# Strassen's scheme for the gate and up projections of two SwiGLU stages

## The chip, the cores and the metric

The kernel runs on one core of a Trainium2 chip. The metric is the device time of one execution in microseconds (us), the median of several runs; smaller is better. A core has a matrix engine (TensorE, PE in the rows; PEld is its loading of weights), VectorE (DVE), ScalarE (ACT), GpSimd (POOL) and SyncE (SP, which here issues most transfers). Each engine works through its own list of instructions in order, and a semaphore holds an instruction until what it reads is there and what it overwrites has been read. Matmuls write PSUM, which has 8 banks of 128x512 fp32; everything else lies in SBUF.

## The reference, cut to what matters

```python
def _swiglu_ffn(x, g_norm, w_gate_up, w_down):
    h = _rms_norm(x, g_norm)
    gate, up = jnp.split(h @ w_gate_up, 2, axis=-1)
    return (jax.nn.silu(gate) * up) @ w_down
...
    for layer in range(DEPTH):
        if layer < N_A:
            x = x + _gmlp_mixer(...)
        else:
            x = x + _chunked_relbias_attention(...)
        x = x + _swiglu_ffn(x, ffn_norm[layer], ffn_w_gate_up[layer], ffn_w_down[layer])
    return _rms_norm(x, final_norm)
```

There are two layers, 1024 tokens, a model width of 1024 and a hidden width of 2816; all is fp32. Layer 0 has the gMLP mixer ahead of its SwiGLU, layer 1 has chunked attention ahead of its SwiGLU.

## The kernel before

The residual stream `x` lies transposed in SBUF: eight tiles `x[d]`, each 128 features by 1024 tokens. A product in fp32 is made of three fp32r matmuls: each operand is split into a rounded part (`hi`, a copy by ScalarE) and the rest (`lo`, a subtraction by VectorE), and `hi*hi`, `hi*lo` and `lo*hi` are summed in PSUM (`split`, line 116; `mm_cols`, line 194; `mm_rows`, line 209).

A SwiGLU stage (`ffn`, line 463) works by blocks `f` of 128 hidden features, 22 of them. For each it multiplies the eight `h` tiles (scaled `x`, split once at the stage's start by `norm_input`, line 185) by a 128x1024 block of gate weights (`wg`) and one of up weights (`wup`). One block is 8 tiles of K x 2 halves of the tokens x 3 matmuls of 128x512, which is 48 for gate and 48 for up. `post` then multiplies both by the broadcast reciprocal norm `rbc` (lines 507 and 510), applies SiLU and the product (lines 514 and 515), and splits the result `y`. After every second `f` the down projection of an earlier pair of blocks runs: 16 units of 6 matmuls, each of which VectorE adds to `x` (line 219). The last pair in layer 0 runs in `rows_late` (line 443; its matmuls are line 455), and the last four blocks in layer 1 run with the final norm.

Weights come through `prep_w` (line 93): a transfer of 512 KB on SP's queue into one of two `wraw` buffers, a split into one of four `whi`/`wlo` pairs, and then `take_w` hands them out in the order of a list. The squares for the norm (`square_add`, line 137) are made by ScalarE and summed by GpSimd (line 149). The norm's own statistics use small fp32 matmuls (lines 169 and 181). The instructions of each engine are ordered by the framework's scheduler and not by the order of the code, so what stands where is shown below from the built programs.

## Time and profile before

| what | value |
|---|---|
| median of 3 runs | 2639.02 us (2638.77 to 2643.23) |
| the profiled execution's own time | 2636.19 us |
| its span in the profile | 2634.4 us |
| TensorE busy | 2578.9 us, 98% of the span |
| VectorE, ScalarE, GpSimd busy | 1456.9, 774.9 and 212.9 us |
| mean granted TensorE clock | 0.994 of full speed |
| moved by transfers | 161.35 MB, 61 GB/s on average |

The span runs from the first to the last instruction of the profile; the execution's own time lies 1.8 us above it, and the median of the runs another 2.8 us above that. The matrix engine's busy time counts overlapping matmuls once, so it says that the engine always has one in flight, not how many finish in a microsecond; for that one counts starts.

### The profile page before, as it was taken

To read this page: it belongs to the slowest core of one execution; us is meant where nothing else is said; L and a number is where in the kernel's file an instruction comes from. 1 tells how busy PE (TensorE), PEld (TensorE's weight loads), DVE (VectorE), ACT (ScalarE), POOL (GpSimd) and SP (SyncE) were. 2 spreads that over 40 slices of the span, in tenths; PEclk is the share of its full clock that TensorE was granted. 3 is DMA by queue.
4 is the path that set the end of the run, shared out by engine and by line. 5 is a ranking of instruction groups with operands and counts; after the bars stand their busy time and mean duration, and the time that the engine had idled before them with its cause. 6 is when DMAs were issued, how large, how long until landed. Compare 5 with 4: busy or idle time off the path is not lost.

```text
span 2634.4 us, 30026 instructions
## 1 busy us (share of the span) xinstructions
PE 2578.9 (98%) x12150; PEld 2138.2 (81%) x12150; DVE 1456.9 (55%) x2388; ACT 774.9 (29%) x1275; POOL 212.9 (8%) x155
## 2 busy tenths in 40 slices
PE   8999999999999999999999999989999999999998
PEld 6888888878888888888777888868888888888887
DVE  6237676774444444444657777788744444444435
ACT  5223322332111111111345555554421111111113
POOL 3001211130000000000410100030200000000001
PEclk9999999999999999999999999999999999999999
DMA  5232222211111111111112222222211111111111
GB/s 192 80 120 68 77 65 68 68 41 41 48 49 48 48 49 48 48 49 49 58 53 67 59 64 59 79 73 70 72 40 49 48 48 48 49 48 48 49 48 64
DMA packets 70538, 161.35 MB, mean 61 GB/s; under 512 B 6016, under 2 KB 34688, under 8 KB 70400
## 3 DMA queue, kind: packets, MB, share of 16 engines
q1 hardware_dynamic: 68096, 155.24, 18.6%
q10 hardware_dynamic: 2304, 4.20, 0.5%
q8 instruction: 95, 1.56, 0.3%
q14 instruction: 43, 0.35, 0.0%
HBM read 134.25 MB, written 16.78 MB: 57 GB/s over the span
## 4 chain that ended last, share of the span: by engine, by line
PE 90%; DVE 5%; ACT 2%; issue 1%; DMA 1%; POOL 1%; DVEq 0%; SPq 0%; ACTq 0%; POOLq 0%
PE ps L204 43%; PE ps L218 22%; PE pj L204 7%; PE pj L218 3%; PE ps L334 2%; PE ps L332 2%; PE ps L333 2%; PE po L756 2%; PE pt L729 2%; PE s L706 1%; PE ps L455 1%; PE s L709 1%; DVE p L713 1%; DVE p L721 1%; DVE kd L675 1%
## 5 line engine op out<-in xcount | busy, mean ns | idle before, releaser
L204 PE MATMUL ps<-hhi,whi 128*128 128x512 f32 x1664 | 655.4, 394 | 0.0
L204 PE MATMUL ps<-hlo,whi 128*128 128x512 f32 x1664 | 648.8, 390 | 2.8 <-DVE hlo L134 2.8
L204 PE MATMUL ps<-hhi,wlo 128*128 128x512 f32 x1664 | 648.2, 390 | 0.0
L117 ACT CAST whi<-wraw 128x1024 fp32r<-128x1024 f32 (+1 forms) x213 | 219.7, 1045 | 1218.2 <-PE ps L204 558.3
L204 PEld LDWEIGHTS ps<-hhi,wlo 128*128 128x128 f32 x1664 | 312.4, 188 | 66.1 <-issue 0.5
L204 PEld LDWEIGHTS ps<-hlo,whi 128*128 128x128 f32 x1664 | 312.9, 188 | 65.4 <-DVE hlo L134 4.1
L204 PEld LDWEIGHTS ps<-hhi,whi 128*128 128x128 f32 x1664 | 312.4, 188 | 61.0 <-issue 0.5
L118 DVE TENSOR_TENSOR wlo<-wraw,whi 128x1024 fp32r<-128x1024 f32 (+1 forms) x213 | 262.9, 1245 | 59.5 <-ACT whi L117 59.4
L510 DVE TENSOR_TENSOR ub<-ps,rbc 128x512 f32<-128x512 f32 x88 | 60.3, 691 | 339.3 <-PE ps L204 339.3
L219 DVE TENSOR_TENSOR x<-x,ps 128x512 f32<-128x512 f32 x272 | 182.5, 684 | 116.2 <-PE ps L218 116.1
L218 PE MATMUL ps<-yhi,whi 128*128 128x512 f32 x544 | 212.6, 391 | 0.0
L218 PE MATMUL ps<-yhi,wlo 128*128 128x512 f32 x544 | 211.7, 389 | 0.0
L218 PE MATMUL ps<-ylo,whi 128*128 128x512 f32 x544 | 211.7, 389 | 0.0
L507 DVE TENSOR_TENSOR ga<-ps,rbc 128x512 f32<-128x512 f32 x88 | 60.3, 691 | 255.4 <-PE ps L204 255.4
L204 PE MATMUL pj<-hhi,whi 128*128 128x512 f32 x368 | 152.9, 415 | 2.0 <-DVE x L458 2.0
L204 PE MATMUL pj<-hlo,whi 128*128 128x512 f32 x368 | 148.2, 403 | 0.7 <-DVE hlo L118 0.7
L204 PE MATMUL pj<-hhi,wlo 128*128 128x512 f32 x368 | 147.8, 402 | 0.0
L219 DVE TENSOR_TENSOR xb<-xb,ps 128x512 f32<-128x512 f32 (+1 forms) x160 | 103.6, 658 | 71.4 <-PE ps L218 71.0
L105 POOL TENSOR_TENSOR wraw<-wraw,gv 128x1024 f32<-128x1024 f32 x24 | 46.4, 1934 | 1014.2 <-DMA wraw<-wv_att 724.5
L218 PEld LDWEIGHTS ps<-yhi,wlo 128*128 128x128 f32 x544 | 102.1, 188 | 21.3
L218 PEld LDWEIGHTS ps<-ylo,whi 128*128 128x128 f32 x544 | 102.2, 188 | 20.7
L218 PEld LDWEIGHTS ps<-yhi,whi 128*128 128x128 f32 x544 | 102.1, 188 | 20.7
(408 smaller groups left out, 4024.0 us busy)
## 6 DMA issues: line engine op xcount, KB each, us to landing
wraw<-wg SPq DMA_DIRECT2D x44, 512.0 KB, 3.3
wraw<-wup SPq DMA_DIRECT2D x44, 512.0 KB, 3.3
wraw<-wd SPq DMA_DIRECT2D x44, 512.0 KB, 3.4
vd<-vt SPq DMA_DIRECT2D x32, 256.0 KB, 2.5
wraw<-wu SPq DMA_DIRECT2D x16, 512.0 KB, 3.5
wraw<-wout SPq DMA_DIRECT2D x16, 512.0 KB, 3.3
vr<-vd SPq DMA_DIRECT2D x32, 256.0 KB, 3.1
wraw<-wv SPq DMA_DIRECT2D x15, 512.0 KB, 3.4
```

What stands on the lines that cost most here:

```text
L117: self.nc.scalar.copy(hi, src)
L118: self.nc.vector.tensor_tensor(lo, src, hi.bitcast(F32), ALU.subtract)
L204: nc.tensor.matmul(ps[s], wt[:, c], ht[:, t], start=(kt == 0 and i == 0), stop=(kt == KT - 1 and i == 2),)
L218: nc.tensor.matmul(o, wt[:, c], yt[:, t], start=(j == 0 and i == 0), stop=(j == last and i == 2))
L219: nc.vector.tensor_tensor(x[d][:, t], x[d][:, t], o, ALU.add)
L332: nc.tensor.matmul(ps[tt], hhi[:, t], whi[:, c], start=(kt == 0), stop=False)
L333: nc.tensor.matmul(ps[tt], hhi[:, t], wlo[:, c], start=False, stop=False)
L334: nc.tensor.matmul(ps[tt], hlo[:, t], whi[:, c], start=False, stop=(kt == KT - 1))
L507: nc.vector.tensor_tensor(t, g[s], rbc[:, c], ALU.mult)
L510: nc.vector.tensor_tensor(b, u[s], rbc[:, c], ALU.mult)
L729: nc.tensor.transpose(tp[:, i * P:(i + 1) * P], pt[:, i * P:(i + 1) * P], self.ident)
L756: nc.tensor.matmul(o, vt[:, kb, j, :], r, start=(i == 0), stop=(i == len(jobs) - 1))
```

## The change

Gate and up of one block `f` are taken as one product of a 2x2 block matrix of weights with a 2x2 block matrix of activations. The rows of the weight matrix are gate (A11, A12) and up (A21, A22), its columns the even and the odd K tiles; the activations are split into even and odd K tiles (rows) and the two halves of the tokens (columns: B11, B12, B21, B22). Winograd's form of Strassen's scheme then makes the four results from seven products in place of eight, with S1 to S4 (sums of weight blocks), T1 to T4 (sums of activation blocks), and sums of the products. The host stores the weights with even K tiles first (`cols2`).

For each `f`, GpSimd makes S1 and S2 (tile `s12`) and S3 and S4 (`s34`) in four operations of 128x512; three and a half tiles of 128x1024 are split in place of two. The seven products have 12 matmuls each, in three PSUM banks; where the scheme sums two products they accumulate in one bank, and ScalarE and VectorE read the bank between them. VectorE makes the remaining sums in four tiles `ac`, `bu`, `gg`, `yy`. The result `y` goes to memory (`yd`).

At the start of a stage `x` goes to memory (`xd`), and `b_tiles` makes seven split tiles of each pair of `x` tiles. The first block (`f` = 0) runs as these tiles come, with seven banks. After the last `f`, `y` and `x` come back from memory and the whole down projection runs as a second pass, with the same matmuls as before. The three matmuls of a product read their operands in the same way as `mm_cols`.

```diff
+    def scratch(self, name, dtype=F32):
+        return self.hx.tile([P, S], dtype, name=name, tag="scr", bufs=3)
...
+    def quad_split(self, q, key, src):
+        w = src.shape[1]
+        hi = self.wp.tile([P, 1024], F32R, name="whi", bufs=self.NW)
+        lo = self.wp.tile([P, 1024], F32R, name="wlo", bufs=self.NW)
+        self.split(hi[:, 0:w], lo[:, 0:w], src)
+        for i, k in enumerate(key):
+            q[k] = (hi[:, i * 512:(i + 1) * 512], lo[:, i * 512:(i + 1) * 512])
...
+    def quad_s12(self, q):
+        nc = self.nc
+        g, u = q["raw"]
+        s12 = self.scratch("s12")
+        nc.gpsimd.tensor_tensor(s12[:, HALF[0]], u[:, HALF[0]], u[:, HALF[1]], ALU.add)
+        nc.gpsimd.tensor_tensor(s12[:, HALF[1]], s12[:, HALF[0]], g[:, HALF[0]], ALU.subtract)
+        q["s12"] = s12
+        self.quad_split(q, ("S1", "S2"), s12)
+    def quad_a(self, q):
+        self.quad_split(q, ("A11", "A12"), q["raw"][0])
+    def quad_s34(self, q, s34=None, split=True):
+        nc = self.nc
+        g, u = q["raw"]
+        s34 = s34 or self.scratch("s34")
+        nc.gpsimd.tensor_tensor(s34[:, HALF[0]], g[:, HALF[0]], u[:, HALF[0]], ALU.subtract)
+        nc.gpsimd.tensor_tensor(s34[:, HALF[1]], g[:, HALF[1]], q["s12"][:, HALF[1]], ALU.subtract)
+        q["s34"] = s34
+        if split:
+            self.quad_split(q, ("S3", "S4"), s34)
+    def quad_a22(self, q):
+        self.quad_split(q, ("A22",), q["raw"][1][:, HALF[1]])
...
+    def b_tiles(self, B, i, xe, xo, ge, go):
+        nc = self.nc
+        t1, t2 = HALF
+        e = self.scratch(f"e{i}")
+        t = self.scratch(f"t{i}")
+        names = {k: self.slot(j, f"b{k}_{i}") for k, j in (
+            ("eh", i), ("el", 4 + i), ("oh", 8 + i), ("ol", 12 + i), ("th", 16 + i), ("tl", 20 + i), ("t4", 24 + i))}
+        eh, el, oh, ol, th, tl, t4 = (names[k] for k in ("eh", "el", "oh", "ol", "th", "tl", "t4"))
+        stt = nc.vector.scalar_tensor_tensor
+        nc.scalar.activation(e, xe, AF.Copy, scale=ge)
+        nc.vector.tensor_tensor(t[:, t1], e[:, t2], e[:, t1], ALU.subtract)
+        stt(t[:, t2], xo[:, t2], go, t[:, t1], ALU.mult, ALU.subtract)
+        stt(e[:, t2], xo[:, t2], go, e[:, t2], ALU.mult, ALU.subtract)
+        self.split(eh, el, e)
+        self.split(th, tl, t)
+        nc.scalar.activation(oh, xo, AF.Copy, scale=go)
+        stt(ol, xo, go, oh.bitcast(F32), ALU.mult, ALU.subtract)
+        stt(e[:, t1], xo[:, t1], go, t[:, t2], ALU.mult, ALU.subtract)
+        self.split(t4[:, t1], t4[:, t2], e[:, t1])
+        for k, (h, l, c) in {"B11": (eh, el, t1), "T3": (eh, el, t2), "B21": (oh, ol, t1), "B22": (oh, ol, t2),
+                             "T1": (th, tl, t1), "T2": (th, tl, t2)}.items():
+            B[k, i] = (h[:, c], l[:, c])
...
+    def product(self, ps, A, B, pairs, start, stop, goes_on=False):
+        nc = self.nc
+        (ahi, alo), key = A, B[0]
+        for i in pairs:
+            c = slice(i * P, (i + 1) * P)
+            bhi, blo = B[1][key, i]
+            for n, (w, h) in enumerate(((ahi, bhi), (ahi, blo), (alo, bhi))):
+                nc.tensor.matmul(ps, w[:, c], h, start=(start and i == pairs[0] and n == 0),
+                                 stop=(stop and i == pairs[-1] and n == 2), skip_group_check=goes_on)
...
+            dp = self.pool(st, f"fdram{layer}", 1, dram=True)
+            xd = dp.tile([KT, P, S], F32, name="xd")
+            yd = dp.tile([FT, P, S], F32, name="yd")
...
+            q = self.quad_load(layer, 0)
+            self.quad_s12(q)
+            self.quad_a(q)
+            self.quad_s34(q, self.slot(23, "s34_0", F32), False)
+            B = {}
+            for i in range(4):
+                for d in (2 * i, 2 * i + 1):
+                    nc.sync.dma_start(xd[d], x[d])
+                self.b_tiles(B, i, x[2 * i], x[2 * i + 1], *(self.gv[:, gain + 2 * i + k:gain + 2 * i + k + 1] for k in range(2)))
+                for d in (2 * i, 2 * i + 1):
+                    self.square_add(sqp or self.hx, acc, x[d], d == 0)
+                if i == 0:
+                    self.quad_split(q, ("S3", "S4"), q["s34"])
+                    self.quad_a22(q)
...
+                return [xplace(4 * (f % 2) + j, f"{n}{f}") for j, n in enumerate(("ac", "bu", "gg", "yy"))]
+            def gate(o, s, src):
+                TT(o[2][:, HALF[s]], src, rbc[:, HALF[s]], mul)
+                nc.scalar.activation(o[2][:, HALF[s]], o[2][:, HALF[s]], AF.Silu)
...
+                y = o[3][:, HALF[s]]
+                TT(y, y, rbc[:, HALF[s]], mul)
+                TT(y, y, o[2][:, HALF[s]], mul)
...
+                    self.product(ps[k], q[A], (b, B), [i], i == 0, i == 3)
...
+            qn = self.quad_load(layer, 1)
+            some(range(4), 0)
+            some(range(4), 1)
+            some(range(4, 7), 0)
+            some(range(4, 7), 1)
+            some(range(7), 2)
+            self.stats(None, bank(), acc, rstd)
+            some(range(7), 3)
+            rbc = self.const.tile([P, S], F32, name="rbc")
+            for s in range(2):
+                self.broadcast(self.hx, bank(), rstd[:, 4 * s:4 * s + 4], rbc[:, HALF[s]], ("scr", 3))
...
+            nc.scalar.copy(ac[:, t1], p1)
+            nc.scalar.copy(ac[:, t2], p5)
+            TT(bu[:, t1], p6, ac[:, t1], add)
+            TT(gg[:, t1], p2, ac[:, t1], add)
...
+            nc.sync.dma_start(yd[0], yy)
+            self.quad_s12(qn)
+            self.quad_a(qn)
+            self.quad_s34(qn)
+            self.quad_a22(qn)
...
+            for f in range(1, FT):
+                more = f + 1 < FT
+                if more:
+                    qn = self.quad_load(layer, f + 1)
...
+                prod(pa, "A11", "B11", True)
+                nc.scalar.copy(ac[:, t1], pa)
+                prod(pb, "S2", "T2", True)
+                TT(bu[:, t1], pb, ac[:, t1], add)
+                prod(pc, "S1", "T1", True)
+                nc.scalar.copy(ac[:, t2], pc)
+                self.quad_s12(qn) if more else self.prep_w()
+                prod(pa, "A12", "B21", stop=True)
+                gate(o, 0, pa)
+                self.quad_a(qn) if more else self.prep_w()
+                prod(pb, "S3", "T3")
+                TT(bu[:, t2], pb, ac[:, t1], add)
+                TT(yy[:, t2], bu[:, t2], ac[:, t2], add)
+                prod(pc, "S4", "B22", stop=True)
+                TT(gg[:, t2], pc, bu[:, t1], add)
+                gate(o, 1, gg[:, t2])
+                up(o, 1, None)
+                self.quad_s34(qn) if more else self.prep_w()
+                prod(pb, "A22", "T4", stop=True)
+                TT(yy[:, t1], pb, ac[:, t1], add)
+                up(o, 0, None)
+                nc.sync.dma_start(yd[f], yy)
+                self.quad_a22(qn) if more else self.prep_w()
+                q = qn
...
+            def load_y(f):
+                j = 16 + 6 * (f // 2 % 2) + 3 * (f % 2)
+                r = self.slot(j, f"y{f}", F32)
+                nc.sync.dma_start(r, yd[f])
+                yt[f] = (self.slot(j + 1, f"y{f}h"), self.slot(j + 2, f"y{f}l"))
+                self.split(*yt[f], r)
...
+            x = []
+            for d in range(KT):
+                x.append(xplace(d, f"x{layer}_{d}"))
+                nc.sync.dma_start(x[d], xd[d])
+            xt[:] = x
+            n = FT if layer == 0 else FT - 4
...
+                ys = [yt.pop(f), yt.pop(f + 1)]
+                if layer == 0 and f == FT - 2:
+                    self.rows_late(psum, ws2, ys, x)
+                else:
+                    self.rows_all(psum, "ps", ws2, ys, x)
                 self.prep_w()
                 self.prep_w()
-                return
+                for k in (f + 4, f + 5):
+                    if k < FT:
+                        load_y(k)
...
+        w = cols(w)
+        k = w.reshape(w.shape[0], P, KT // 2, 2, P).transpose(0, 1, 3, 2, 4)
+        return np.ascontiguousarray(k).reshape(w.shape)
...
+        o[f"wg{l}"] = cols2(gu[:, :FF])
+        o[f"wup{l}"] = cols2(gu[:, FF:])
```

**VectorE, one block `f` in the middle of the first stage.** Before, from the pair's two `wlo` splits to the end of `post`:

```order
L118 TENSOR_TENSOR wlo<-wraw,whi 128x1024 x2
L507 TENSOR_TENSOR ga<-ps,rbc 128x512 x2
L118 TENSOR_TENSOR wlo<-wraw,whi 128x1024
L510 TENSOR_TENSOR ub<-ps,rbc 128x512 x2
L515 TENSOR_TENSOR ub<-ub,ga 128x512
L118 TENSOR_TENSOR wlo<-wraw,whi 128x1024
L118 TENSOR_TENSOR ylo<-ub,yhi 128x512
L515 TENSOR_TENSOR ub<-ub,ga 128x512
L118 TENSOR_TENSOR ylo<-ub,yhi 128x512
```

And now, from the split of `s12` (shown as `s` with a number) to the last split of that block's weights:

```order
L118 TENSOR_TENSOR wlo<-s_5320,whi 128x1024
L598 TENSOR_TENSOR gg_5276<-ps,rbc 128x512
L118 TENSOR_TENSOR wlo<-wraw,whi 128x1024
L674 TENSOR_TENSOR bu_5275<-ps,ac_5274 128x512
L675 TENSOR_TENSOR yy_5277<-bu_5275,ac_5274 128x512
L604 TENSOR_TENSOR yy_5277<-yy_5277,rbc 128x512
L677 TENSOR_TENSOR gg_5276<-ps,bu_5275 128x512
L598 TENSOR_TENSOR gg_5276<-gg_5276,rbc 128x512
L118 TENSOR_TENSOR wlo<-s_5376,whi 128x1024
L605 TENSOR_TENSOR yy_5277<-yy_5277,gg_5276 128x512
L682 TENSOR_TENSOR yy_5277<-ps,ac_5274 128x512
L118 TENSOR_TENSOR wlo<-wraw,whi 128x512
```

The splits for the next block now stand between the sums of this one, and the last split, which frees the buffer for the next `wup` transfer, stands behind eight sums and three other splits.

**ScalarE, the start of the first stage.** Before, the tail of `norm_input` (`hhi` is the rounded part of one scaled `x` tile):

```order
L133 ACTIVATE hhi_4455<-x_97,gv 128x1024
L148 ACTIVATE sq<-x_97 128x512
L133 ACTIVATE hhi_4465<-x_98,gv 128x1024
L117 CAST whi<-wraw 128x1024
L148 ACTIVATE sq<-x_98 128x512 x2
L133 ACTIVATE hhi_4475<-x_99,gv 128x1024
L148 ACTIVATE sq<-x_99 128x512 x2
L133 ACTIVATE hhi_4485<-x_100,gv 128x1024
L148 ACTIVATE sq<-x_100 128x512 x2
L117 CAST whi<-wraw 128x1024
```

And now, from the last squares to the first block's operands (`bth` and `beh` are rounded parts that the first products read):

```order
L148 ACTIVATE sq<-x_99 128x512
L527 ACTIVATE e_4420<-x_93,gv 128x1024
L148 ACTIVATE sq<-x_99 128x512
L117 CAST whi<-s_4404 128x1024
L117 CAST whi<-wraw 128x1024
L117 CAST bth_4426<-t_4421 128x1024
L117 CAST whi<-s_0_4415 128x1024
L117 CAST whi<-wraw 128x512
L527 ACTIVATE e_4460<-x_95,gv 128x1024
L117 CAST beh_4422<-e_4420 128x1024
L533 ACTIVATE boh_4536<-x_100,gv 128x1024
```

`beh` of the first pair now stands behind four copies of weights, two of which (those of tiles `s`) wait for GpSimd.

**GpSimd, the same place.** Now, from the sums of squares through the first block's S sums to those of the second block:

```order
L149 TENSOR_TENSOR rbc<-rbc,sq 128x512 x10
L496 TENSOR_TENSOR s_4404<-wraw 128x512
L508 TENSOR_TENSOR s_0_4415<-wraw 128x512
L497 TENSOR_TENSOR s_4404<-s_4404,wraw 128x512
L149 TENSOR_TENSOR rbc<-rbc,sq 128x512
L509 TENSOR_TENSOR s_0_4415<-wraw,s_4404 128x512
L149 TENSOR_TENSOR rbc<-rbc,sq 128x512 x3
L496 TENSOR_TENSOR s_4716<-wraw 128x512
L508 TENSOR_TENSOR s_4727<-wraw 128x512
```

Before, GpSimd had the sums of squares alone here, ten of them. The first block's S sums now stand behind ten of the fourteen, and the remaining four stand among and behind them.

## Rows read from the trace of the kernel before

**Rows 1.** The page: span, and part 1 for TensorE.
```profile
span 2634.4 us, 30026 instructions
...
PE 2578.9 (98%) x12150; PEld 2138.2 (81%) x12150; DVE 1456.9 (55%) x2388; ACT 774.9 (29%) x1275; POOL 212.9 (8%) x155
```

**Rows 2.** The page, part 4: the chain that ended last, by engine.
```profile
PE 90%; DVE 5%; ACT 2%; issue 1%; DMA 1%; POOL 1%; DVEq 0%; SPq 0%; ACTq 0%; POOLq 0%
```

**Rows 3.** Busy time by stretch: one in the first SwiGLU stage.
```profile
800.00:900.00 100.00, 100.00 (x443) 82.85 (x442) 38.20 (x51) 17.29 (x23) 0.00 (x0) 1.00 0.15 48
```

**Rows 4.** Timeline of TensorE: start, duration; two starts that lie 34 matmuls apart.
```profile
870.01 0.39 PE L204 MATMUL ps<-hlo,whi 128*128 128x512 f32 x1
...
877.72 0.39 PE L204 MATMUL ps<-hhi,wlo 128*128 128x512 f32 x1
```

**Rows 5.** Timeline of TensorE around the first SwiGLU stage.
```profile
546.13 0.39 PE L455 MATMUL ps<-yhi,whi 128*128 128x512 f32 x1
...
585.23 1.84 PE L169 MATMUL ps<-ones,rbc 128*128 128x1 f32 x16
...
593.86 1.02 PE L181 MATMUL ps<-dg,ones 128*128 128x512 f32 x2
...
1293.20 0.39 PE L455 MATMUL ps<-yhi,wlo 128*128 128x512 f32 x1
```

**Rows 6.** Line 204 from 1860 to 1960 us: min/median/max ns, first and last start.
```profile
L204 PEld LDWEIGHTS ps<-hhi,whi x96: 187/188/192, 1891.3 to 1959.6; 128*128 128x128 f32 x96
```

**Rows 7.** Groups of VectorE, shapes apart: count, busy us, mean ns.
```profile
L118 DVE TENSOR_TENSOR wlo<-wraw,whi 128x1024 fp32r<-128x1024 f32 x211 | 261.5, 1250 | 54.6 <-ACT whi L117 54.4
L219 DVE TENSOR_TENSOR x<-x,ps 128x512 f32<-128x512 f32 x272 | 182.5, 684 | 116.2 <-PE ps L218 116.1
...
L118 DVE TENSOR_TENSOR hlo<-x,hhi 128x1024 fp32r<-128x1024 f32 x8 | 16.3, 2073 | 0.0
```

**Rows 8.** Timeline of VectorE, 558 to 592 us, merged rows.
```profile
558.68 6.64 DVE L134 SCALAR_TENSOR_TENSOR hlo<-x,gv,hhi 128x1024 fp32r<-128x1024 f32 x3
...
567.48 4.26 DVE L458 TENSOR_TENSOR x<-x,ps 128x512 f32<-128x512 f32 x7
...
588.11 0.17 DVE L160 TENSOR_TENSOR nt<-ms,rstd 128x8 f32<-128x8 f32 x1
588.31 0.17 DVE L161 SCALAR_TENSOR_TENSOR nt<-nt,rstd 128x8 f32<-128x8 f32 x1
```

**Rows 9.** Groups of GpSimd, shapes apart: count, busy us, mean ns.
```profile
L149 POOL TENSOR_TENSOR facc<-facc,sq 128x512 f32<-128x512 f32 x3 | 3.9, 1290 | 699.8 <-PE ps L455 697.1 <-ACT sq L148 2.7
```

**Rows 10.** Line 149 on GpSimd: min/median/max ns of one.
```profile
L149 POOL TENSOR_TENSOR rbc<-rbc,sq x44: 1262/1613/2286, 9.8 to 1892.7; 128x512 f32<-128x512 f32 x44
```

**Rows 11.** Timeline of GpSimd at the start of each SwiGLU stage.
```profile
557.22 14.03 POOL L149 TENSOR_TENSOR rbc<-rbc,sq 128x512 f32<-128x512 f32 x8 [12.40 <-issue]
...
1875.74 18.24 POOL L149 TENSOR_TENSOR rbc<-rbc,sq 128x512 f32<-128x512 f32 x10 [99.44 <-ACT sq L148]
```

**Rows 12.** Groups of ScalarE, shapes apart: count, busy us, mean ns.
```profile
L117 ACT CAST whi<-wraw 128x1024 fp32r<-128x1024 f32 x211 | 218.5, 1049 | 1215.6 <-PE ps L204 558.3 <-PE ps L218 410.6 <-issue 174.0
...
L133 ACT ACTIVATE hhi<-x,gv 128x1024 fp32r<-128x1024 f32 x8 | 9.1, 1140 | 1.1 <-DVE x L458 1.1
```

**Rows 13.** DMA issues: count, KB each, median us from issue to landing.
```profile
wraw<-wg SPq DMA_DIRECT2D x44, 512.0 KB, 3.3
...
wraw<-wq SPq DMA_DIRECT2D x8, 512.0 KB, 6.0
```

**Rows 14.** TensorE by 2 us: busy, matmuls, granted clock (1.00 is 2.4 GHz).
```profile
1294.00:1296.00 2.00, 0.55 (x3) 1.00 0.93 320
1296.00:1298.00 2.00, 1.49 (x4) 0.62 0.67 250
...
1308.00:1310.00 2.00, 0.48 (x4) 1.00 0.00 0
...
1314.00:1316.00 2.00, 2.00 (x7) 0.50 0.00 0
```

More of the change, by code (lines that the diff above doesn't have):

```diff
@@ L262, in run @@
             return self.dump(x)
-        self.ffn(x, 1, None)
+        x = self.ffn(x, 1, None)
         if stop == "ffn1":
@@ new lines, in ffn, with some @@
+            order = (("A11", "B11"), ("S2", "T2"), ("S1", "T1"), ("A12", "B21"), ("S3", "T3"), ("S4", "B22"), ("A22", "T4"))
+            ps = [bank() for _ in order]
+            def some(ks, i):
+                for k in ks:
+                    A, b = order[k]
+                    self.product(ps[k], q[A], (b, B), [i], i == 0, i == 3)
[4 more added lines that the diff above has]
+            some(range(4, 7), 1)
@@ new lines, in ffn @@
+            yt = {}
+            def load_y(f):
[4 more added lines that the diff above has]
+                self.split(*yt[f], r)
+            for f in range(4):
+                load_y(f)
+            x = []
+            for d in range(KT):
+                x.append(xplace(d, f"x{layer}_{d}"))
+                nc.sync.dma_start(x[d], xd[d])
```

159 lines of the change are left out of this document (69 added, 90 removed).

## The prediction

> **What bounds the kernel now.** I read the page first: TensorE is busy 98% of the span, VectorE 55%, and the chain that ended last is TensorE for 90% [rows 1, 2]. Busy time does not say how dense the matmuls are, so I read a window inside the first SwiGLU stage: 443 matmuls in 100 us, no idle time, while VectorE does 38 us of work and GpSimd none [rows 3]. Two starts that lie 34 matmuls apart are 7.72 us apart, 0.227 us each [rows 4]; 100/443 is the same. I use 0.2267.
>
> A stage has 22 x 96 gate and up matmuls and 22 x 48 down matmuls, 3168, which is 718 us at this pace. The first stage begins when `rows_late` of the mixer ends: it starts at 546.1 and has 96 matmuls, so at 567.9; its own last matmul starts at 1293.2 [rows 5]. That is 725 us, so before loses about 7 us in the stage, at its start, where the mixer's last additions, the scaling of `x` and the norm come. So inside a stage only fewer matmuls help, and a change may lose as much as it likes on VectorE until TensorE waits.
>
> **What it removes.** Seven products of 12 replace 96 matmuls for each block: 84. Over 22 blocks and two stages 528 fewer, 528 x 0.2267 = **-119.7 us**. Down keeps its matmuls.
>
> **The middle of a stage.** One block is now 84 x 0.2267 = 19.04 us of TensorE. For it VectorE has 3.5 splits at 1.25 and eleven sums of 128x512 at about 0.68, the price of the addition that reads PSUM [rows 7]: 4.4 + 7.5 = 11.9 us. ScalarE has 3.5 copies at 1.05 and four half-size operations at some 0.57 [rows 12]: 6 us. GpSimd has four sums at 1.29 [rows 9]: 5.2 us. None comes near 19.
>
> A loop could still be longer than a block. There are two `wraw` buffers, and both are held by one block's weights. The last split of a block's `wup` (`lo` of A22) frees its buffer; only then does the next transfer start: 3.3 us [rows 13]; GpSimd makes three sums before `s12` is whole, 3.9 us [rows 9]; ScalarE rounds it, 1.05 [rows 12]; VectorE goes from `lo` of `s12` to `lo` of A22, which in the order shown is 3.5 splits and eight sums, 4.4 + 5.4 us [rows 7]. That is 18.1 us, and an engine starts 0.03 us after another operation ends [rows 8], so 18.2. It is under 19.04 by 0.8 us. TensorE would not stop at once even there: the first operation it misses is the sum that empties the bank which A22 T4 needs, some 2 us ahead of need. I take **+3 us** in all for small waits in 40 such blocks (bounds 0, and the contended loop below).
>
> The prices may be worse in company. Beside GpSimd the 128x1024 `hlo` took 2.07 us, and three of them 2.2 each, against 1.25 for `wlo`; an addition that reads PSUM kept its 0.61 there [rows 7, 8]. GpSimd's sum took 1.29 alone and 1.75 to 1.82 in company, 2.29 at most [rows 9 to 11]. In the loop GpSimd's first three sums lie where VectorE has little to do, so the low prices are the nearer ones. The Trainium skill ("SBUF — State Buffer", section "Who interferes with whom") speaks against the change here: an operation of VectorE with two inputs from SBUF and one of GpSimd contend for a port pair under an exclusive lock, so one waits for the other's end, while a PSUM input leaves it free. The trace agrees about the PSUM additions. By the lock the only meeting in the loop is GpSimd's fourth sum with `lo` of `s12`: an estimate by it is 18.3 us for the loop, and 2572 would stand.
>
> **The start of the first stage.** Here the trace shows no such operations, and I build it from the three orders. GpSimd starts ten of the sums of squares at 557.2 [rows 11]; at 1.75 they end at 574.8. Then come the S sums, a sum of squares among them, each 1.3 to 1.75: `s34` is whole at about 582. ScalarE's queue makes `beh`, which the first product reads, wait behind the copy of that `s34`: 582 + 1.05 + 0.5 + 2 x 1.14 = 586 [rows 12]. TensorE, free at 568, waits 18 us.
>
> From there VectorE sets the pace. `b_tiles` costs it, for one pair, three splits, one half split and four half sums, 3.75 + 0.6 + 2.7 = 7 us [rows 7]. Three pairs remain, 21 us, with 4.4 us for the first block's weights and some 2.6 for the statistics and their short dependent operations: 28 us, to 614. The first block's matmuls go in between, since seven banks take them as pairs come. Then nine sums (about 6 us) stand in VectorE's order ahead of `lo` of the second block's `s12` (1.25): 621. The second block may run 6 matmuls before it; the other 78 take 17.7 us, to 639. From 568 that is 71 us, in which two blocks alone would be 38.1: 33 lost, of which before lost 7. **+26 us** (bounds: 19 with GpSimd's sums at 1.29, which brings the first product 7 us forward; 34 with every `lo` beside GpSimd at 2.07).
>
> **The start of the second stage.** Gate and up matmuls start at 1891.3 [rows 6]; the attention's order ahead of it is unchanged. GpSimd runs its ten sums from 1875.7 at 1.82 [rows 11], the fourteen would end 10 us past 1891. The `x` tiles come one by one there, so the first pair is ready early, the first block's weights are split in VectorE's waits, and VectorE needs four pairs and the statistics, 31 us, then 7 us as above, then 17.7: 55.6 after 1891.3. Less 38.1 it is 17.5, less the 4 us that I allow before at the same place (an estimate, half of the first stage's 7): **+13.5 us** (10 to 18).
>
> **The clock.** After the gaps around 1295 and 1309, in which TensorE was busy 0.5 of 2 us, the granted clock fell to 0.62 and 0.50, that is to its lower level, 1.2 GHz, for some us [rows 14]. A first block that runs in pieces has such gaps, and the statistics another. Each us at half clock costs half a us while TensorE is the bound. I take **+8 us** for both stages (bounds 3 and 15), on the ground that one or two stretches of 3 to 7 us fall into the time when TensorE is needed.
>
> **The second pass.** One pair of `f` is 96 matmuls, 21.8 us, against 16 additions and four splits on VectorE, 10.9 + 5 = 16 us [rows 7]: TensorE stays the bound. `y` and `x` are loaded ahead. The change between passes, with the first `y` to fetch (3.3 to 6.0 us [rows 13], weights of down lying ready), may cost 1 us in each stage: **+2** (0 to 8). Storing `y` and loading it adds 23 MB a stage to SP's queue, where the transfer engines are busy 0.15 of the time [rows 3]: nothing, because transfers hide behind 19 us of matmuls; without that cover each transfer costs 3.3 us.
>
> **The sum.** -119.7 + 3 + 26 + 13.5 + 8 + 2 = -67.2 us. The profiled execution took 2636.2, so 2569; the median of the runs lies 2.8 us above that execution, so **2572 us**.
>
> **Rivals.**
>
> *The loop is contended.* GpSimd at 1.75 (+1.4 us) and `lo` of `s12` at 2.07 (+0.8) make 20.4 us of the 18.2: 1.4 us over a block, 40 times, about +54 in place of the +3. Without the +3 the forecast is 2569, so 2623, and half of that excess gives 2596. For it: these are the prices of both engines in company. Against it: GpSimd's sums wait for a transfer while VectorE waits for products. Chance 0.2.
>
> *The starts overlap better.* GpSimd at 1.29, 19 and 10 us in place of 26 and 13.5, clock 3, no waits in the middle: -119.7 + 19 + 10 + 3 + 2 = -85.7, or 2553. For it: engines that wait for one another leave each other alone. Against it: the mixer's last additions keep VectorE busy beside GpSimd just there [rows 8]. Chance 0.15.
>
> *The buffer loop becomes the bound: slower.* Its place is the wait of the `wup` transfer for `lo` of A22. It decides when the loop exceeds 19.04 + 70/40 = 20.8 us. With a transfer of 6.0 (+2.7), GpSimd at 2.29 (+3.0) and `lo` at 2.07 (+0.8) it is 24.7 us, 40 x 5.7 = +226: 2795. For it: `wq` transfers of the same size did take 6.0 [rows 13]. Against it: `wg` ones took 3.3 in the stage itself, where the load of the transfer engines is low. Chance 0.05.
>
> *It does not do what it says.* The built programs hold 528 matmuls fewer; chance 0.
>
> **How the numbers follow.** The forecast itself has 0.6; its bounds are 2572 - 3 - 7 - 3.5 - 5 = 2553 with everything kind, and 2572 + 8 + 4.5 + 7 + 6 = 2598 with everything unkind. Towards the contended loop I go to 2620, nearly its whole, and towards the better starts to 2545, some us below it. That leaves out the slower rival, the rest of the contended loop and what I have not seen, 0.2. Within 0.2% of before, about what a measurement of this kernel can tell from no change (5 us), I give 0.03; slower 0.05; faster 0.92.
>
> **What would show it.** In windows in the middle of a stage 443 matmuls in 100 us at clock 1.00, with a period of 19.0 us from one block's first matmul to the next. TensorE's idle time gathered in two places: some 18 us after 568 with the first product near 586, the second block done near 639; the like, smaller, after 1891. GpSimd's S sums at 1.29 in the middle, and `lo` of A22 followed by a transfer of 3.3 us. The forecast is wrong if those windows show under 430 matmuls, with the chain going through the `wup` transfer and GpSimd (the contended loop); if idle time at the starts is far from 33 and 17 us; or if the granted clock stays low beyond the first two blocks.

## The result

The changed kernel takes 2563.48 us, median of 4 runs (2561.52 to 2565.33), against 2638.89 before (2637.02 to 2643.23): a ratio of 0.9712, 95% interval 0.9695 to 0.9729. The prediction was 2572, with a range of 2545 to 2620. The profiled execution took 2565.3, its span 2563.5.

The page of the changed kernel, span, part 1 and the engines of the chain, to read beside [rows 1, 2]:

```profile
span 2563.5 us, 30266 instructions
...
PE 2483.5 (97%) x11622; PEld 2051.7 (80%) x11622; DVE 1709.2 (67%) x2696; ACT 910.5 (36%) x1431; POOL 449.2 (18%) x339
...
PE 88%; DVE 6%; ACT 2%; issue 1%; POOL 1%; DMA 1%; DVEq 0%; SPq 0%; ACTq 0%; POOLq 0%
```

TensorE has 528 instructions fewer and VectorE 252 us more work, and still TensorE is busy 97% of a shorter span. The window in the middle of the first stage is the one to compare with [rows 3]: 443 matmuls again, while VectorE's work rose from 38 to 58 us and GpSimd's from 0 to 28.

```profile
800.00:900.00 100.00, 100.00 (x443) 82.81 (x442) 58.14 (x77) 30.86 (x41) 27.83 (x22) 1.00 0.26 89
```

What it lost lies at the starts. TensorE's waits from 560 to 660 us, the three longest (in all, times, longest; `beh` and `bel` are the rounded part and the rest of an even activation tile, `bth` the rounded part of a T tile, `whi` that of a weight tile):

```profile
PE ps L550 <- ACT beh L117: 15.0, 1, 15.0
PE ps L550 <- ACT whi L117: 5.2, 1, 5.2
PE ps L550 <- ACT bth L117: 1.0, 1, 1.0
```

And its timeline: the last matmul of the mixer, the first product, the first matmul of the second block, the last of the stage, the last of the attention, and a wait in the second start.

```profile
569.16 0.39 PE L442 MATMUL ps<-yhi,wlo 128*128 128x512 f32 x1
584.55 0.79 PE L550 MATMUL ps<-beh,whi 128*128 128x512 f32 x1 [15.00 <-ACT beh L117]
...
622.96 0.79 PE L550 MATMUL ps<-beh,whi 128*128 128x512 f32 x1 [5.24 <-ACT whi L117]
...
1264.61 0.39 PE L442 MATMUL ps<-y21h,wlo 128*128 128x512 f32 x1
...
1856.44 0.39 PE L218 MATMUL pj<-o7h,wlo 128*128 128x512 f32 x1
...
1859.99 0.80 PE L550 MATMUL ps<-bel,whi 128*128 128x512 f32 x1 [2.93 <-DVE bel L118]
```

The same four marks (last matmul of mixer, first stage, attention, and the end) cut every profiled execution into pieces. The table is worked out from them, 0.23 us being added for the last matmul itself; the medians are over all runs of a kernel.

| kernel | median | first stage | attention | second stage and final norm |
|---|---|---|---|---|
| before | 2638.89 | 725.5 | 598.1 | 742.9 |
| before, a second profile | 2642.21 (one run) | 725.5 | 600.3 | 746.2 |
| changed | 2563.48 | 695.4 | 591.8 | 706.8 |
| twelve matmuls more per block | 2679.00 | 751.3 | 598.4 | 758.9 |
| without A22 T4 | 2546.25 | 690.0 | 594.7 | 692.2 |
| without A22 T4, own buffers | 2451.85 | 639.1 | 598.0 | 644.3 |
| first weights early | 2563.32 | 688.2 | 591.2 | 709.6 |
| no sums of squares | 2550.27 | 686.6 | 588.9 | 701.9 |
| one plain block | 2554.63 | 684.0 | 592.5 | 702.1 |
| two plain blocks | 2559.45 | 682.3 | 595.1 | 711.4 |
| all blocks plain | 2651.55 | 729.3 | 595.7 | 755.6 |
| one plain block, reordered | 2559.69 | 684.1 | 593.2 | 710.6 |
| two plain blocks, reordered | 2550.58 | 678.4 | 599.4 | 707.2 |

So the change gained 30.1 us in the first stage and 36.1 in the second, 66.2 together. Another 6.3 came in the attention, which the change leaves alone; the time up to the mixer's end was 1.5 longer.

Two things limit what this table can tell. Each row is one profiled execution, which can lie some us off the median: 5.6 below it with one plain block, 3.3 above it with two plain blocks, reordered. And the last column holds 3 to 5 us that come and go without any change. In the final norm TensorE waits 1.64 us for GpSimd in every profile. From the end of this wait to the end of the span it is 36.7 us in the first profile of before, 40.1 in the second and 40.2 in the changed kernel; the first matmul behind it, and a window 4 us later, in this order:

```profile
2597.68 0.38 PE L577 MATMUL ps<-ones,facc 128*128 128x1 f32 x2 [1.64 <-POOL facc L149]
2602.00:2606.00 4.00, 4.00 (x32) 3.74 (x31) 3.28 (x11) 1.19 (x4) 1.00 (x1) 1.00 0.00 0
...
2600.31 0.38 PE L577 MATMUL ps<-ones,facc 128*128 128x1 f32 x2 [1.64 <-POOL facc L149]
2604.00:2608.00 4.00, 4.00 (x20) 4.00 (x20) 1.14 (x7) 0.00 (x0) 0.00 (x0) 0.50 0.00 0
...
2523.34 0.38 PE L750 MATMUL ps<-ones,facc 128*128 128x1 f32 x2 [1.64 <-POOL facc L149]
2527.00:2531.00 4.00, 4.00 (x20) 4.00 (x20) 1.15 (x7) 0.02 (x1) 0.00 (x0) 0.50 0.01 2
```

The granted clock (ahead of the last two columns) stayed at 1.00 in the first and fell to 0.50, its lower level of 1.2 GHz, in the others, though the first two are the same kernel. Over the thirteen profiles this end took 36.7 us six times (before once, twelve matmuls more, both without A22 T4, one plain block, all blocks plain) and 40.0 to 41.3 seven times.

### The profile page after: what moved, and what is told of

Same layout as the page of the kernel before. It is cut to its first block, busy times and chain, and to the rows that moved or that the text cites. A ratio compares the mean times of both kernels' runs of the same rounds, so it can differ in the third digit from the quotient of the medians.

```text
span 2563.5 us, 30266 instructions
## 1 busy us (share of the span) xinstructions
PE 2483.5 (97%) x11622; PEld 2051.7 (80%) x11622; DVE 1709.2 (67%) x2696; ACT 910.5 (36%) x1431; POOL 449.2 (18%) x339
## 4 chain that ended last, share of the span: by engine, by line
PE 88%; DVE 6%; ACT 2%; issue 1%; POOL 1%; DMA 1%; DVEq 0%; SPq 0%; ACTq 0%; POOLq 0%
PE ps L550 31%; PE ps L218 23%; PE pj L204 8%; PE ps L204 7%; PE pj L218 3%; PE po L930 2%; PE ps L321 2%; PE ps L319 2%; PE ps L320 2%; PE pt L903 2%; PE s L880 1%; PE ps L442 1%; PE s L883 1%; DVE wlo L118 1%; POOL rbc L149 1%
## 5 line engine op out<-in xcount | busy, mean ns | idle before, releaser
L219 DVE TENSOR_TENSOR x<-x,ps 128x512 f32<-128x512 f32 (+1 forms) x432 | 281.6, 675 | 169.5 <-PE ps L218 169.0
L118 DVE TENSOR_TENSOR wlo<-wraw,whi 128x1024 fp32r<-128x1024 f32 (+1 forms) x213 | 240.9, 1141 | 55.9 <-ACT whi L117 55.9
L550 PE MATMUL ps<-beh,whi 128*128 128x512 f32 x352 | 138.8, 397 | 23.2 <-ACT beh L117 15.0
L550 PE MATMUL ps<-bth,whi 128*128 128x512 f32 x352 | 139.9, 400 | 2.5 <-ACT bth L117 2.4
L550 PE MATMUL ps<-bel,whi 128*128 128x512 f32 x352 | 138.4, 393 | 3.6 <-DVE bel L118 3.6
L550 PE MATMUL ps<-bth,wlo 128*128 128x512 f32 x352 | 139.8, 398 | 1.6 <-DVE wlo L118 1.6
L550 PE MATMUL ps<-btl,whi 128*128 128x512 f32 x352 | 140.7, 400 | 0.0
L550 PE MATMUL ps<-boh,whi 128*128 128x512 f32 x352 | 138.1, 392 | 0.0
L550 PE MATMUL ps<-bol,whi 128*128 128x512 f32 x352 | 137.9, 392 | 0.0
L550 PE MATMUL ps<-boh,wlo 128*128 128x512 f32 x352 | 137.8, 391 | 0.0
L550 PE MATMUL ps<-beh,wlo 128*128 128x512 f32 x352 | 137.5, 390 | 0.0
```

Source lines behind the costliest of these rows:

```text
L118: self.nc.vector.tensor_tensor(lo, src, hi.bitcast(F32), ALU.subtract)
L219: nc.vector.tensor_tensor(x[d][:, t], x[d][:, t], o, ALU.add)
L550: nc.tensor.matmul(ps, w[:, c], h, start=(start and i == pairs[0] and n == 0), stop=(stop and i == pairs[-1] and n == 2), skip_group_check ...
```

## The experiments

### Twelve matmuls more per block

```diff
                 prod(pb, "A22", "T4", stop=True)
+                prod(bank(), "A22", "T4", True)
```

> The changed kernel with twelve matmuls more in every block but the first (the last product is run once more into a bank that nobody reads): 96 matmuls per block as before the change, with all else of the scheme left in. Theory (TensorE alone sets the pace of the middle): 21 blocks x 2 stages x 12 x 0.2267 = +114.3 us on 2563.5, so 2678, and 443 matmuls in 100 us in the middle. Rival (some of the removed matmuls were hidden behind another engine): less than +105.

Measured: 2679.0 us (2676.47 to 2679.61), 1.0147 of before (1.0132 to 1.0162), 115.5 above the changed kernel. The window is the same to a hundredth on TensorE:

```profile
800.00:900.00 100.00, 100.00 (x443) 82.80 (x442) 52.13 (x66) 27.87 (x37) 25.41 (x20) 1.00 0.20 71
```

The total fits the theory, but by the table 6.6 us of it are the attention's. The stages grew by 55.9 and 52.1, not 57.1 each. In the second, 3.4 of the missing 5.0 are the final norm's, whose clock did not fall in this execution; what is left, 1 to 2 us in each stage, lies at the starts. Matmuls in the middle have their full price; the kernel has no other limit there at 84 or at 96.

### The last product left out, with shared and with own buffers

The first run drops the product A22 T4 and its tiles. The second also gives `wup` two buffers, in the place of the T4 tiles.

```diff
-                prod(pb, "A22", "T4", stop=True)
 # second run, in quad_load
-            r = self.wp.tile([P, 1024], F32, name="wraw", bufs=2)
+            if name == "wg":
+                r = self.wp.tile([P, 1024], F32, name="wraw", bufs=2)
+            else:
+                r = self.slot(24 + f % 2, "wraw", F32)
```

> The changed kernel without its last product (A22 T4) and without the T4 tiles; this part of the computation is left out. 72 matmuls per block, 16.3 us of TensorE, while the weights' loop (last split of a block's up weights, transfer, three sums of GpSimd, rounding, VectorE's way to the next last split) has 18.2 us by the prediction's prices and 18.5 with the 3.6 us that a transfer took in the changed kernel. Theory: the loop now sets the pace, 18.2 to 18.6 us per block, so 0.4 to 0.8 us less than 19.04 in 40 blocks, 16 to 34 us, and about 10 us less at the two starts: 2520 to 2537; TensorE shows 390 matmuls in 100 us. First rival (the loop is much shorter than I worked out): TensorE stays the bound, 2.72 us less in 42 blocks, 114 us, and 10 at the starts: 2439. Second rival (the loop runs at the contended prices, 20.3): slower blocks than now, over 2563.

> As the run without the last product, also leaving out A22 T4, and with two buffers of their own for the up weights (in the place of the T4 tiles), so that a transfer no longer waits for the last split of the block before. Theory (the buffer is what closes the loop): TensorE's 16.3 us per block, 443 matmuls in 100 us, 2439. Rival (the period comes from the sums on VectorE, or from GpSimd, and not from the buffer): the same time as with the shared buffers.

Measured: 2546.25 us (2543.41 to 2547.09) and 2451.85 (2449.92 to 2458.04). The windows, first shared, then own:

```profile
800.00:900.00 100.00, 90.96 (x376) 72.99 (x375) 58.10 (x78) 32.05 (x44) 27.58 (x22) 0.95 0.26 79
```

```profile
800.00:900.00 100.00, 100.00 (x443) 82.81 (x442) 75.17 (x92) 35.51 (x50) 40.64 (x26) 1.00 0.31 100
```

With shared buffers 376/72 = 5.2 blocks pass in 100 us, 19.1 us each, although TensorE needs 16.3. One turn of the loop, in the timeline of all engines of that run:

```profile
802.21 1.33 DVE L118 TENSOR_TENSOR wlo<-s,whi 128x1024 fp32r<-128x1024 f32 x1 [7.52 <-ACT whi L117]
...
811.32 0.68 DVE L118 TENSOR_TENSOR wlo<-wraw,whi 128x512 fp32r<-128x512 f32 x1
...
812.03 0.33 SPq L480 DMA_DIRECT2D wraw<-wup  x1
...
816.38 1.29 POOL L496 TENSOR_TENSOR s<-wraw 128x512 f32<-128x512 f32 x1 [13.91 <-DMA wraw<-wup]
...
818.87 1.27 POOL L497 TENSOR_TENSOR s<-s,wraw 128x512 f32<-128x512 f32 x1
820.16 1.04 ACT L117 CAST whi<-s 128x1024 fp32r<-128x1024 f32 x1 [7.62 <-POOL s L497]
...
821.24 1.31 DVE L118 TENSOR_TENSOR wlo<-s,whi 128x1024 fp32r<-128x1024 f32 x1 [7.85 <-ACT whi L117]
```

From `lo` of `s12` to the next it is 19.03 us: VectorE 9.8, the transfer 4.35, GpSimd 3.76, ScalarE 1.04, and the handing over. This is the loop of the prediction, step by step, but 0.8 us longer than its 18.2; the transfer's 4.35 in place of 3.3 makes more than the difference. With own buffers it is gone and TensorE sets the pace. That run ended 13 us above its forecast. In its profile the attention was 6.2 longer than in the changed kernel, the two changes between passes had waits of 1.0 and 1.4, the starts gave some 4 of the 10 us expected of them (the first product of the first stage waited 19.0 us), and the final norm was 3.5 shorter.

The first expectation, 18.2 to 18.6, was right on the mechanism and short on its size, so that its total, 2520 to 2537, was missed. For the change it means that little below 19 us per block is to be had with these buffers and this order. In the changed kernel itself the transfer of the same window took 3.8 us, from its issue to GpSimd's start:

```profile
817.90 0.33 SPq L480 DMA_DIRECT2D wraw<-wup  x1
...
821.67 1.29 POOL L496 TENSOR_TENSOR s<-wraw 128x512 f32<-128x512 f32 x1 [13.93 <-DMA wraw<-wup]
```

The same sum with this transfer is 18.5, an estimate, with about half a us to spare.

### The first block's weights early

```diff
                 ws2 = [self.take_w(), self.take_w()]
+                self.first_block(0, "hlo7", "hlo6")
                 self.rows_late(psum, ws2, [yt.pop(14), yt.pop(15)], x)
 ...
             for t in (4, 6):
+                if t == 6:
+                    self.first_block(1, "hlo3", "hlo2")
```

`first_block` loads, sums and splits what `ffn` did at its start.

> The changed kernel with the first block's weight loads, its four sums on GpSimd and its splits written ahead of the last down products of the mixer and of the attention; in the built program GpSimd makes the four sums before the sums of squares, and VectorE's and ScalarE's splits of S1, S2 and A11, A12 stand ahead of the last additions. Theory (after the first product VectorE's work sets how long a start lasts; the first product waits for GpSimd): the first product comes some 9 us earlier, near 575, and the second block ends some 8 to 10 us earlier at the first stage and 6 to 8 at the second: 2563.5 - 16 = 2547 (2541 to 2553). Rival (the start is set by the x tiles, the squares and the statistics, and the weights are made in waits anyway): the first product comes earlier, the second block does not, 2560 to 2564.

Measured: 2563.32 us (2560.33 to 2564.07), as the changed kernel. The first product of the first stage came 8.8 us earlier:

```profile
575.71 0.80 PE L557 MATMUL ps<-beh,whi 128*128 128x512 f32 x1 [6.06 <-ACT beh L117]
```

`lo` of the second block's `s12` started at 616.86 against 624.34, and the first stage was 7.2 us shorter, near the theory's 8 to 10. The second stage was not (709.6 against 706.8, with the final norm alike): there TensorE waited 5.5 us for `bel` where it had waited 2.9. So the theory held in one stage of two and its total, 2547, was missed. The two profiled executions lie 5.0 us apart (2560.33 and 2565.28), the medians 0.2, so a gain of this size in one stage is at the limit of what totals can tell.

### No sums of squares

```diff
-                    self.square_add(sqp or self.hx, acc, x[d], d == 0)
+                    if d == 0:
+                        self.square_add(sqp or self.hx, acc, x[d], True)
```

> The changed kernel without 14 of the 16 squares of x tile halves at the start of each SwiGLU stage and without GpSimd's sums of them; this leaves out most of the norm's statistics. In the changed kernel VectorE's operations beside GpSimd took about twice their time there (bel 2.33 against 1.22, a half sum 1.75 against 0.68). Theory (VectorE sets the end of a start, and GpSimd slows it): the second block ends 8 us earlier in each stage, and the first product comes earlier by the sums that stood ahead of the first block's: 2563.5 - 16 = 2547 (2540 to 2553). Rival (VectorE's excess lies in time in which it would wait for x tiles anyway): 2560 to 2564.

Measured: 2550.27 us (2542.95 to 2552.96), 13 less, as the theory had it. The first stage was 8.8 us shorter, the second 4.9, against 8 each; the attention, which the edit leaves alone, was 2.9 shorter in this profile. What GpSimd does to VectorE is plain in the changed kernel's timeline. The first line began just before an operation of GpSimd; then come the same forms, first beside GpSimd, then with GpSimd idle:

```profile
578.31 1.23 DVE L118 TENSOR_TENSOR wlo<-s,whi 128x1024 fp32r<-128x1024 f32 x1 [2.23 <-ACT whi L117]
579.46 2.29 DVE L118 TENSOR_TENSOR wlo<-wraw,whi 128x1024 fp32r<-128x1024 f32 x1
...
584.48 1.21 DVE L118 TENSOR_TENSOR wlo<-s,whi 128x1024 fp32r<-128x1024 f32 x1
...
588.43 1.77 DVE L535 SCALAR_TENSOR_TENSOR e<-x,gv,t 128x512 f32<-128x512 f32 x1
...
596.90 0.75 DVE L535 SCALAR_TENSOR_TENSOR e<-x,gv,t 128x512 f32<-128x512 f32 x1
```

and GpSimd's own, one with VectorE idle for most of it, two beside it:

```profile
577.16 1.26 POOL L149 TENSOR_TENSOR rbc<-rbc,sq 128x512 f32<-128x512 f32 x1
578.39 2.27 POOL L509 TENSOR_TENSOR s<-wraw,s 128x512 f32<-128x512 f32 x1
580.62 2.24 POOL L149 TENSOR_TENSOR rbc<-rbc,sq 128x512 f32<-128x512 f32 x1
```

Each side grows by about 1.0 us, which is nearly one operation of the other. The rule that the prediction weighed (the Trainium skill, "SBUF — State Buffer", section "Who interferes with whom": one waits for the other's end) fits this better than two engines that are both slowed. The lines above show it: the operation at 578.31 was first and kept its 1.23, and each of the next three, at 578.39, 579.46 and 580.62, ended 1.1 us after the other engine's had ended, which is about what it takes alone. The run leaves out ScalarE's squares too, so not all of the 13 us need be GpSimd's; the two were not tried apart.

### Plain first blocks

One or two first blocks of a stage by eight products; their tiles need 2.5 us of VectorE for a pair in place of 7, and the T tiles are made beside these products. The core of the first run:

```diff
+            for i in range(4):
+                for k, (A, A2, b, b2) in enumerate((("A11", "A12", "B11", "B21"), ("A11", "A12", "B12", "B22"),
+                                                    ("A21", "A22", "B11", "B21"), ("A21", "A22", "B12", "B22"))):
+                    self.product(pg[k], q[A], (b, B), [i], i == 0, False)
+                    self.product(pg[k], q[A2], (b2, B), [i], False, i == 3)
+            for i in range(4):
+                self.b_rest(B, i, x[2 * i], x[2 * i + 1], gains[2 * i], gains[2 * i + 1])
+            self.stats(None, bank(), acc, rstd)
```

> The changed kernel with the first block of each stage by eight products of the plain activations (24 matmuls for each of its four halves, 96 in all), for which VectorE needs only 2.5 us of splits for a pair of x tiles; the T tiles are made while these products run. Theory (a start lasts as long as VectorE needs for its tiles, and TensorE can work beside that): 2.7 us more matmuls in each stage, but the second block ends 16 us earlier in the first stage (628 in place of 644.7) and 6 us earlier in the second: 2563.5 - 22 = 2541 (2533 to 2552). Rival (VectorE has the same work before the second block, so that this block comes no earlier): 2563 to 2569.

> The changed kernel with the first two blocks of each stage by eight products of the plain activations; the T tiles are made during both, T4 last. Theory (as for one plain block): both blocks take 43.5 us of matmuls without much waiting; the third block begins near 618 in the first stage, where the changed kernel had it at 644.7, and some 13 us earlier in the second: 2563.5 - 38 = 2525 (2517 to 2540). Rival (contention with GpSimd and the longer order of VectorE take it back): 2545 to 2565.

Measured: 2554.63 us (2549.01 to 2559.37) with one, 2559.45 (2558.78 to 2560.89) with two. Both are above the theory's ranges; the second lies in its rival's. By stages one plain block gave 11.4 and 4.7 us in place of 16 and 6, and 3.5 of the 4.7 are the final norm's; two gave 13.1 in the first and lost 4.6 in the second. With one, TensorE stood before the broadcast of the norm, whose operand `dg` VectorE made behind all T tiles:

```profile
607.00 3.78 PE L181 MATMUL ps<-dg,ones 128*128 128x512 f32 x4 [12.52 <-DVE dg L178]
```

With two, this wait was 3.0 us, but a later one came, in the third block:

```profile
644.06 1.22 PE L597 MATMUL ps<-bt,whi 128*128 128x512 f32 x2 [4.85 <-DVE bu L729]
```

The sum `bu` stands behind `lo` of `s12`, that behind a `wup` transfer issued at 631.01, because `lo` of A22 came late, at 630.3. It is the buffer loop again. Two more runs tested both waits. The first writes the statistics into the first block and the broadcast ahead of the last T tiles; the second does the same for two plain blocks and orders the second block's products so that S3, S4 and A22 are split earlier.

```diff
 # one plain block
             for i in range(4):
+                if i == 3:
+                    self.stats(None, bank(), acc, rstd)
 ...
+            rest(0)
+            rest(1)
+            self.quad_a(qn)
 # (broadcast, gate and up of the first block)
+            rest(2)
+            rest(3)
 # two plain blocks: order of the second block's halves
-            for s in (1, 0):
-                    for k in range(2):
+            for k, s in ((0, 1), (0, 0), (1, 1), (1, 0)):
```

> As the run with one plain first block, with three things written earlier: the statistics' small matmuls inside the first block, the broadcast and the first block's gate ahead of the last two pairs of T tiles, and the second block's A11, A12 splits ahead of them. Theory (the 12.5 us in which TensorE waited for the broadcast there were mostly time that VectorE needs for the T tiles anyway): the second block ends only 2 to 5 us earlier in each stage, 2545 to 2552 against 2554.6. Rival (the wait for the broadcast was the cause by itself): 10 us less in each stage, 2535.

> As the run with two plain first blocks, with the second block's products ordered so that the third block's S3, S4 and A22 are split some 10 us earlier and the statistics inside the first block. Theory (the loop through the up weights' buffer has no slack against 19.04 us, so that the late first turn in the run before, 12 us, came back as waits of later blocks): the first stage ends some 12 us earlier than in that run and the second some 15: 2559 - 27 = 2532 (2522 to 2545). Rival (its extra time came from something else, VectorE's longer work on T4 or the clock): 2553 to 2562.

Measured: 2559.69 us (2557.01 to 2562.74) and 2550.58 (2546.51 to 2553.90); neither lies in a range that was expected. With one block the wait for `dg` fell from 12.5 to 1.9 us and the first stage stayed at 684.1 (684.0): TensorE then waited for roundings (4.7 us) and a copy (3.2 us) on ScalarE, while VectorE, from 588 to 619 us, stood still for 3. The rival is refuted: the wait by itself cost nothing, since VectorE's work lasts as long either way. The second stage was 8.5 us longer than without the reordering: 3.3 are the final norm's, and why its start lost the other 5 is not known.

With two blocks the first stage was 3.9 us shorter and the second 4.2, a third of what was expected. The loop's first turn came 5.05 us earlier (transfer at 625.96 against 631.01), and its wait was still there, 4.28 us in place of 4.85:

```profile
638.66 1.22 PE L597 MATMUL ps<-bt,whi 128*128 128x512 f32 x2 [4.28 <-DVE bu L731]
```

The third block itself came earlier, so the loop was late by as much again. That it is this loop that makes the wait is read from the rows; that the rest of the missing gain has the same cause is not shown. At 0.9656 of before (0.9639 to 0.9673) this is the fastest complete kernel here, 0.5% under the changed one.

### All blocks plain

```diff
+                for k, (A, A2, b, b2) in enumerate((("A11", "A12", "B11", "B21"), ("A11", "A12", "B12", "B22"),
+                                                    ("A21", "A22", "B11", "B21"), ("A21", "A22", "B12", "B22"))):
+                    self.product(pg[k], q[A], (b, B), range(4), True, False)
+                    self.product(pg[k], q[A2], (b2, B), range(4), False, True)
```

> All blocks of both stages by eight products, 96 matmuls for each block as before the change, with no sums of weights or products; what stays of the change is that x and y pass through memory and that the whole down projection is a second pass. Theory (this part costs what the sum of the prediction gave it, 2 us, or less): the time of before the change, 2639 to 2643. Rival (the passage through memory costs something that the shorter middle of the changed kernel hid): over 2650.

Measured: 2651.55 us (2650.30 to 2653.63), 1.0047 of before (1.0032 to 1.0062). The number is the rival's, its reason is not. TensorE waits for nothing from 700 to 1290 and from 1960 to 2590, which holds the stores and loads of `y` and both changes between passes:

```profile
700.00:900.00 200.00, 200.00 (x884) 1.00 0.22 77
2100.00:2300.00 200.00, 200.00 (x884) 1.00 0.21 71
```

The loss against the first profile of before is 3.8 us in the first stage and 12.7 in the second, at the starts (the final norm took the same 36.7 us): in the second, 4.2 for `bel`, 4.0 for `dg`, and a broadcast that TensorE runs by itself. Before, matmuls stood around these steps.

```profile
1926.65 3.78 PE L181 MATMUL ps<-dg,ones 128*128 128x512 f32 x4 [4.00 <-DVE dg L178]
```

### The kernel before, a second time

> The kernel before, unchanged, for a second profile. The attention between the two stages, whose code and order the change leaves alone, took 598.1 us before and 591.8 us after, and 588.9 to 598.4 in the kernels tried so far. Theory (its time wanders by itself with the phase at which it begins): a value in that span, not needfully 598.1, and the two stages as before within 1 us. Rival (the change made it shorter): 598 again.

Measured: 2642.21 us. The attention took 600.3, the first stage 725.5 again, the second 746.2, 3.3 more than in the first profile. All of this lies behind the wait in the final norm, where the clock fell this time (40.1 us to the end against 36.7). So the theory's bound of 1 us held for the first stage and for the second up to the final norm. Over the thirteen profiles the attention, with its own code unchanged, took 588.9 to 599.4 in variants of the changed kernel and 598.1 and 600.3 in the kernel before. That the 6.3 us are chance is likely from this and not shown: both profiles of before lie at the upper end.

## Why the prediction was right

**What bounds the kernel, and what is removed.** Right. 443 matmuls in 100 us with 84, with 96 and, given buffers, with 72 per block: each matmul has its 0.2267 us, and 528 fewer are 119.7.

**The middle, +3.** Measured 0: TensorE's waits from 645 us to the end of the first stage, and from 1919 to 2290, are none. The loop was the right thing to fear and its margin was put at 0.8; with the transfer as measured it is about 0.5, an estimate, and 0.0 with the turn of 19.03 in the run without A22 T4.

**The second pass, +2.** Measured 0 in the changed kernel, as in the run with plain blocks.

**The starts, +26 and +13.5, and the clock, +8.** 22 x 132 matmuls at 0.2267 are 658.3 us. The first stage took 695.4, so 37.1 were lost, against 725.5 - 718.2 = 7.3 before: 29.8. In the second stage 706.8 - 658.3 = 48.5 against 742.9 - 718.2 = 24.7: 23.8, but 3.5 of these are the final norm's, by its clock, and not the change's. Together 53.5 (119.7 less the 66.2 gained) where the sum had 47.5, and 50 without the final norm.

In the first stage the steps came as forecast, 1.5 us being the mixer's later end: first product at 584.6 (586), the second block's `lo` of `s12` at 624.3 (its end was put at 621, so 620), the block's end at 644.7 (639 without the clock). The 3 us that stay at `s12` lie where VectorE works beside GpSimd: three of the sums ahead of it took 1.20, 1.74 and 1.75 in place of 0.68. The upper bound had this for the splits alone. The second block's first matmul came only at 622.96, because its own A11 was rounded behind `s12` on ScalarE; the six matmuls that the prediction put ahead of `lo` of `s12` just fitted in.

In the second stage the term was 13.5. In the first 80 us of the stage the kernel before started 337 of the stage's own matmuls and the changed one 247; at 0.2267 that leaves 3.6 and 24.0 us lost, so 20.4. The 4 us credited to before were about right in size, if not by their reason: TensorE did not wait there, but the norm's small matmuls (16 for the statistics, four for the broadcast) take 2.8. What was mis-sized is VectorE's way to the second block. The two starts of `lo` of `s12`:

```profile
624.34 1.21 DVE L118 TENSOR_TENSOR wlo<-s,whi 128x1024 fp32r<-128x1024 f32 x1
...
1897.66 1.21 DVE L118 TENSOR_TENSOR wlo<-s,whi 128x1024 fp32r<-128x1024 f32 x1
```

The second lies 41.0 after the attention's last matmul had ended, where 38 to its end, so 36.8, was forecast: 4.2. Most of the rest is the low clock.

The low clock came where it was expected and cost less. Windows of 4 us after the two long waits of the first start (TensorE's busy time, then the other engines, the granted clock ahead of the last two columns):

```profile
584.00:588.00 4.00, 2.77 (x6) 1.76 (x7) 4.00 (x4) 2.59 (x4) 1.79 (x2) 0.50 0.13 51
588.00:592.00 4.00, 4.00 (x11) 3.13 (x10) 4.00 (x5) 0.62 (x1) 1.65 (x1) 0.50 0.40 131
592.00:596.00 4.00, 3.88 (x15) 2.66 (x15) 3.51 (x5) 3.15 (x3) 0.00 (x0) 0.91 0.00 0
...
624.00:628.00 4.00, 4.00 (x13) 2.98 (x12) 4.00 (x6) 2.81 (x5) 0.00 (x0) 0.65 0.00 0
```

At 0.50 (1.2 GHz) starts lie 0.43 us apart, so each matmul costs 0.2 more. The second block's second, third and seventh matmul of the first stage, and the seventh of the second stage:

```profile
623.55 0.63 PE L550 MATMUL ps<-bel,whi 128*128 128x512 f32 x1
623.97 0.63 PE L550 MATMUL ps<-bth,whi 128*128 128x512 f32 x1
...
625.68 0.72 PE L550 MATMUL ps<-bth,wlo 128*128 128x512 f32 x1
...
1898.93 0.79 PE L550 MATMUL ps<-bth,wlo 128*128 128x512 f32 x1 [1.56 <-DVE wlo L118]
```

Most of the low clock lies in time in which VectorE is the bound and costs nothing. The six matmuls ahead of the seventh ran while `lo` of `s12` was being made and would have waited for it; only the slow ones from the seventh on count, 3 in the first stage and 11 in the second, 0.6 and 2.2 us. Besides, VectorE waited 1.3 us in each start for the copy of a product that had run slow (`gg` at 613.87, `bu` at 1887.78). Together that is some 5.4 of the 8, an estimate from these rows.

**The sum.** Stages: -119.7 + 53.5 = -66.2, forecast -67.2. That these are 1.0 apart is in part luck: the starts, the clock and the final norm cost 6.0 more than the 47.5, and the 5 us for the middle and the second pass were not needed. The rest of the way from 2569 to the profiled 2565.3 is the attention's -6.3 and +1.5 before the mixer's end. The median then lies 1.8 us below the profiled execution, where the prediction added 2.8. So most of the 8.5 us between 2572 and 2563.5 are effects that the prediction did not speak of.

**The rivals.** The loop never became the bound, and the starts overlapped worse, not better, than the kind case had it.

## What to carry to other kernels

When a change removes work from the engine that is the bound, price the removal at that engine's pace in its dense stretch, and then go through the places where it will stand idle, starts above all: here they gave back some 42% of the gain (50 of 119.7). A buffer that is refilled late in a block closes a loop over transfer and several engines; add it up even where every engine is half idle, since it sets a floor on the block that no further saving on the bound gets under. An engine's wait for one operation is not worth its length when the engine behind it is busy throughout.

## What the runs showed that was not expected

A VectorE operation with two operands in SBUF and a GpSimd operation of 128x512 that meet both take about 1.0 us longer (2.29 for 1.21, 2.27 for 1.26), as if one stood still for the other. Behind one and the same wait of 1.64 us in the final norm the granted clock fell in seven profiles and stayed at 1.00 in six, the kernel before being among both, which is worth 3 to 5 us. The attention's time, with code and order unchanged, spread over 11 us (588.9 to 600.3) between kernels that differ elsewhere.
